# A hybrid attention layer on one core: compression MLP in two halves with its weights ahead of q_b's, first projections' banks emptied by ACT alone, k's norm weights made earlier

## The chip, the core and the metric

The kernel runs on one core of a Trainium2 chip. The metric is the device time of one execution in microseconds; before the change the median of three runs is 331.12 us (330.75 to 331.83).

## What is computed

One decoder layer on a sequence of 512 positions with 1024 channels in float32. Two groups of 8 heads of 64 attend side by side: group A with a sliding window and sinks, group B with three branches (compressed, selected, window). Cut to what matters here:

```python
h = rms_norm(x, norm_gain) * (1 + scale) + shift            # scale, shift, gate from c @ w_ada
proj = h @ w_in      # q_a|k_a|v_a|z_a | q_b|kc|vc|ks|vs|kw|vw|z_b|g_b
qa = qk_norm(q_a, q_gain_a) * qscale;  ka = qk_norm(k_a, k_gain_a)
o_a = banded_gqa(qa, ka, v_a, 128, bias_a, sinks)
k_cmp = qk_norm(compress_blocks(kc, pos_k, w_cmp_k1, w_cmp_k2), k_gain_cmp)
v_cmp = compress_blocks(vc, pos_v, w_cmp_v1, w_cmp_v2)
# compress_blocks: 31 overlapping blocks of 32 positions, silu(flat @ w1) @ w2, flat has 32*64 = 2048 inputs
o_b = sum of three gated branches (compressed, selected, window) with q_b
out = x + gate * (concat(o_a * silu(z_a), o_b * silu(z_b)) @ w_out)
```

## The kernel before

**Split products.** Each projection is made of three matmuls per tile of 128 channels: activations and weights are split into a rounded high part and the rest (`hh`, `hl` and `wh`, `wl`), and the products high x high, high x low and low x high are summed in a PSUM bank. For the weights, `split` (L161) lets ACT copy the high part (L171) and DVE subtract (L172). A weight group comes in two loads of 128x4x256 (`raw`) and is split in four parts; a split of a load's last part calls `load_next` (L147), which issues the next load of the list `raw_order` (L140 to L144) on SP's queue. The ring of raw buffers has ten places after the build, and a load waits on SP until the buffer's last reader is done; what stands behind it on SP waits too.

**Phase one** (L300 to L434) makes `h` and the first projections (q, k and v of group A) tile by tile: for each of 8 tiles DVE or PE sums the modulation (`mod_dve`, `mod_pe`), PE turns it into a column (`mod_col`, L260), DVE and ACT make `hh` and `hl`, and `first_proj` (L291) adds 24 matmuls into six banks: `sq` 0 to 3 (q of the four blocks of 128 positions) and `skv` 0 and 1 (k and v). An instruction order written by hand (`in_order`) holds in this phase. At its end DVE makes `kg` (L428 to L433), the products of q's and k's gains.

**Emptying the banks** (L437 to L451): ACT squares q (L441), copies v (L445) and half of q (L450); DVE copies k (L444) and the other half of q (L448). `prep_a` (L570) sums the squares (L573), and for k squares the copy on ACT (`sumsq`, L511, L514); `rnorm` makes the inverse root (L521 and L101 to L108); `k_scale` (L547) scales k with `kg` and splits it, PE transposes it (L560), ACT and DVE copy the transposes (L564, L565); `q_scale` (L524) does the like for q (L527 to L544).

**Phase two.** A scheduler orders each engine's instructions from the program's order and its own costs; `block()` (L495) only fixes PE's order within attention. The program is written as one stream of projections (`gen1`, `gen2`: kv_cmp, kv_sel, kv_win_g, q_b, z) that `run` (L970) advances by an amount per attention step; small tasks hang on the stream as `posts`, of which one step is taken per stream step. `cmp_mlp` (L607) is such a task: 16 steps of the 2048 inputs, each with one matmul for k and one for v of 64 columns (L614), in four quarters of four steps with one task step after each; after each quarter it calls `load_next` twice. Its sums stay in one of the two score banks (`ph`) until L622 has read them. Its weights are the loads `cmp0` (k) and `cmp1` (v), a quarter each: two quarters of both stand ahead of q_b's first two loads in `raw_order`, two behind.

## Time and profile before

| | us |
|---|---|
| median of three runs | 331.12 |
| profiled execution, whole | 331.1 |
| its span, first to last instruction | 328.9 |
| PE busy | 320.3 (97%) |
| DVE busy | 225.5 (69%) |
| ACT busy | 197.8 (60%) |
| matmuls | 2304 |

Times of instructions are counted from the span's start; 2.2 us of the execution lie outside the span. The granted TensorE clock is full throughout. Matmuls overlap: a matmul of 256 columns shows 0.28 us, but the next starts 0.12 us after it, so lengths of PE work are read from start to start. "Idle" in a row is the time in which the engine did nothing before it, and the name behind the arrow is what ended it.

### The profile page before, as it was taken

To read this page: it belongs to the slowest core of one execution; us is meant where nothing else is said; L and a number is where in the kernel's file an instruction comes from. 1 tells how busy PE (TensorE), PEld (TensorE's weight loads), DVE (VectorE), ACT (ScalarE), POOL (GpSimd) and SP (SyncE) were. 2 spreads that over 40 slices of the span, in tenths; PEclk is the share of its full clock that TensorE was granted. 3 is DMA by queue.
4 is the path that set the end of the run, shared out by engine and by line. 5 is a ranking of instruction groups with operands and counts; after the bars stand their busy time and mean duration, and the time that the engine had idled before them with its cause. 6 is when DMAs were issued, how large, how long until landed. Compare 5 with 4: busy or idle time off the path is not lost.

```text
span 328.9 us, 6232 instructions
## 1 busy us (share of the span) xinstructions
PE 320.3 (97%) x2304; PEld 262.9 (80%) x2304; DVE 225.5 (69%) x661; ACT 197.8 (60%) x478; POOL 4.6 (1%) x22
## 2 busy tenths in 40 slices
PE   8999999999999899999999999999999999999995
PEld 3577888879999779999977778678788788788884
DVE  3557697999896248787899799686576784543320
ACT  5674645656887355994967758878487586421200
POOL 1000000000000000000000000000000000000000
PEclk9999999999999999999999999999999999999999
DMA  7999966600050883122042260535240022152321
GB/s 222 388 408 410 397 222 182 247 0 3 3 159 0 276 282 117 32 65 67 32 129 81 78 229 3 190 123 200 66 128 2 0 67 64 34 161 69 123 64 64
DMA packets 31062, 44.27 MB, mean 135 GB/s; under 512 B 1767, under 2 KB 23399, under 8 KB 31033
## 3 DMA queue, kind: packets, MB, share of 16 engines
q1 hardware_dynamic: 29880, 41.79, 37.4%
q10 hardware_dynamic: 1152, 2.10, 2.2%
q8 instruction: 18, 0.29, 0.4%
q14 instruction: 12, 0.09, 0.1%
HBM read 41.74 MB, written 2.14 MB: 133 GB/s over the span
## 4 chain that ended last, share of the span: by engine, by line
PE 83%; DVE 7%; ACT 6%; DMA 2%; issue 1%; SPq 0%; ACTq 0%; DVEq 0%
PE pj L489 31%; PE sq L296 7%; PE pj L479 7%; PE s L878 6%; PE po L953 6%; PE pt L936 4%; PE skv L297 3%; PE skv L322 3%; PE pt L926 3%; PE s L614 2%; DMA raw<-in_w_cmp 2%; ACT pa L890 2%; PE pj L229 2%; PE po L959 1%; PE pj L715 1%
## 5 line engine op out<-in xcount | busy, mean ns | idle before, releaser
L171 ACT ACTIVATE wh<-raw 128x512 fp32r<-128x512 f32 (+1 forms) x52 | 31.4, 631 | 38.0 <-PE pj L489 31.5
L172 DVE TENSOR_TENSOR wl<-raw,wh 128x512 fp32r<-128x512 f32 (+1 forms) x52 | 35.1, 692 | 12.2 <-ACT wh L171 10.6
L479 PE MATMUL pj<-wl,hh 128*128 128x256 f32 (+1 forms) x128 | 36.9, 288 | 0.8 <-DVE wl L172 0.8
L479 PE MATMUL pj<-wh,hh 128*128 128x256 f32 (+1 forms) x128 | 37.1, 291 | 0.1
L479 PE MATMUL pj<-wh,hl 128*128 128x256 f32 (+1 forms) x128 | 37.0, 289 | 0.0
L890 ACT ACTIVATE pp<-pp,nm 128x256 f32<-128x256 f32 (+2 forms) x48 | 29.3, 612 | 10.9 <-DVE nm L883 10.8
L489 PE MATMUL pj<-hh,wh 128*128 128x512 f32 x80 | 32.4, 406 | 0.0
L489 PE MATMUL pj<-hl,wh 128*128 128x512 f32 x80 | 31.8, 397 | 0.0
L489 PE MATMUL pj<-hh,wl 128*128 128x512 f32 x80 | 31.6, 395 | 0.0
L883 DVE CUSTOM_DVE_ANT_0 pp<-s,bias 128x256 f32<-128x256 f32 (+2 forms) x48 | 25.4, 551 | 8.6 <-PE s L878 8.4
L489 PE MATMUL pj<-yh,wh 128*128 128x512 f32 x64 | 25.5, 399 | 0.0
L489 PE MATMUL pj<-yh,wl 128*128 128x512 f32 x64 | 25.3, 395 | 0.0
L489 PE MATMUL pj<-yl,wh 128*128 128x512 f32 x64 | 25.2, 394 | 0.0
L479 PEld LDWEIGHTS pj<-wl,hh 128*128 128x128 f32 x128 | 24.1, 188 | 1.3 <-DVE wl L172 1.0
L479 PEld LDWEIGHTS pj<-wh,hh 128*128 128x128 f32 x128 | 24.0, 188 | 1.0 <-issue 0.5
L479 PEld LDWEIGHTS pj<-wh,hl 128*128 128x128 f32 x128 | 24.1, 188 | 0.6 <-issue 0.6
L878 PE MATMUL s<-kTb,qs 128*128 128x256 f32 (+2 forms) x96 | 23.2, 359 | 0.0
L1037 DVE SCALAR_TENSOR_TENSOR fin<-pj,gate,xr 128x512 f32<-128x512 f32 x8 | 6.0, 751 | 24.6 <-PE pj L489 24.6
L911 DVE TENSOR_SCALAR pp<-pp,rr,grev 128x256 f32<-128x256 f32 (+2 forms) x48 | 21.0, 476 | 0.5
L883 DVE CUSTOM_DVE_ANT_0 pa<-s,bias,nsink 128x256 f32<-128x256 f32 (+1 forms) x32 | 14.2, 448 | 10.1 <-PE pj L479 4.4
L927 ACT COPY ptT<-pt 128x512 f32<-128x512 f32 (+1 forms) x28 | 15.3, 547 | 7.2 <-PE pt L926 7.0
L489 PEld LDWEIGHTS pj<-hh,wh 128*128 128x128 f32 x80 | 15.0, 188 | 4.7 <-issue 2.1
(241 smaller groups left out, 724.9 us busy)
## 6 DMA issues: line engine op xcount, KB each, us to landing
ada_ring<-in_w_ada_ss SPq DMA_DIRECT2D x16, 512.0 KB, 7.2
raw<-in_w_cmp SPq DMA_DIRECT2D x8, 512.0 KB, 6.7
raw<-in_w_gate SPq DMA_DIRECT2D x8, 512.0 KB, 3.8
raw<-in_w_o SPq DMA_DIRECT2D x8, 512.0 KB, 3.9
wst_ring<-in_w_qkv_a SPq DMA_DIRECT2D x8, 384.0 KB, 8.1
xTp<-in_xT SPq DMA_DIRECT2D x8, 256.0 KB, 5.4
bias<-line_d SPq DMA_DIRECT2D x8, 256.0 KB, 4.1
raw<-in_w_q_b SPq DMA_DIRECT2D x4, 512.0 KB
```

The costliest lines, as they stand in the source:

```text
L171: ACT.activation(wh, src, AF.Copy)
L172: DVE.tensor_tensor(wl, src, wh.bitcast(F32), op=OP.subtract)
L296: PE.matmul(pj_q[tb], lt, w[:, 0:512], start=f, stop=l, skip_group_check=True)
L479: PE.matmul(bank[:, t * n:(t + 1) * n], h[:, tb * 128:(tb + 1) * 128], w[:, k % 2, :], start=k == 0 and m == 0, stop=k == 7 and m == 2)
L489: PE.matmul(bank, w, h, start=k == 0 and m == 0, stop=k == 7 and m == 2)
L878: PE.matmul(ps, qs[h][:, 128 * i:128 * i + 128], k[:, hl_, lo:lo + w], start=hl_ == 0, stop=hl_ == 1)
L883: DVE.tensor_tensor_reduce(out=P[:, g, 0:w], in0=ps, in1=bt, scale=1.0, scalar=init, op0=OP.add, op1=OP.min, accum_out=nm[:, g:g + 1])
L890: ACT.activation(P[:, g, 0:e], P[:, g, 0:e], AF.Exp, bias=nm[:, g:g + 1], scale=-1.0, accum_out=dn[:, g:g + 1])
L911: DVE.tensor_scalar(v, v, rr[:, g:g + 1], gates[:, g, br:br + 1], op0=OP.mult, op1=OP.mult)
L927: ACT.copy(T[:, :, 0:nb, :], rev(pt[:, 0:2 * nb * 128].rearrange("p (g b q) -> p g b q", g=2, b=nb)))
L936: PE.transpose(pt[:, b * 128:(b + 1) * 128], P[:, g, b * 128:(b + 1) * 128], ident)
L953: PE.matmul(o[64 * g:64 * g + 64, 128 * i:128 * i + 128], vb[:, 64 * g:64 * g + 64], sl["T"][g][:, b, :], start=first_of and b == 0, stop= ...
```

## The change

- `raw_order`: all eight loads of the MLP's weights stand ahead of q_b's.
- `cmp_mlp` runs in two halves of eight steps, each one uncut `block()`; `load_next` is called twice after each fourth step, within the block. Before the second half it passes eight task steps (`WAIT_M`).
- Emptying: ACT does all of it. It squares the four q banks, squares k straight from its two banks into the new tile `ksq`, copies k, then q, then v. `prep_a` sums `ksq`; the squaring of k's copy is gone.
- The six operations on `kg` stand at the head of phase one's sixth round (`k == 5`), and `kg` becomes a part of the tile `rest`.

The diff, from the old kernel to the new:

```diff
@@ -27,7 +27,7 @@
 GW = 280
 AHEAD = 6
 NT2 = 38
-WAIT_L = 4
+WAIT_L, WAIT_M = 4, (0, 8)
 PER_A, PER_B = 3.6, (3.5, 1.6, 7)
 ND = (24, 8, 3)
 NR = 4
@@ -111,7 +111,7 @@
 
     first = con.tile([128, 168], F32, name="first")
     cT, prm, ident = first[:, 0:8], first[:, 8:40], first[:, 40:168]
-    rest = con.tile([128, 960], F32, name="rest")
+    rest = con.tile([128, 1216], F32, name="rest")
     sml, anti = rest[:, 0:416], rest[:, 416:544]
     pos = rest[:, 544:576].rearrange("p (a b) -> p a b", a=2)
     w2 = rest[:, 576:832].rearrange("p (a b d) -> p a b d", a=2, b=2)
@@ -126,7 +126,7 @@
     hl = [T2(F32R, f"hl{k}") for k in range(8)]
     gacc = con.tile([128, D], F32, name="gacc")
     line_d = dram.tile([2, 8, LINE], F32, name="line_d")
-    kg = con.tile([128, 4, HD], F32, name="kg")
+    kg = rest[:, 960:1216].rearrange("p (a d) -> p a d", a=4)
     nsink = con.tile([128, 8], F32, name="nsink")
     sc_col = con.tile([128, 8], F32, name="sc_col")
     prm1 = con.tile([128, 8], F32, name="prm1")
@@ -138,9 +138,8 @@
 
 
     raw_order = [(g, h) for g in ("kv_cmp", "kv_sel", "kv_win_g") for h in range(2)]
-    raw_order += [(f"cmp{kv}", q) for q in range(2) for kv in range(2)] + [("q_b0", 0), ("q_b0", 1)]
-    raw_order += [(f"cmp{kv}", q) for q in range(2, 4) for kv in range(2)]
-    raw_order += [(g, h) for g in ("q_b1", "z_a0", "gate0", "z_a1", "gate1", "z_b0", "gate2", "z_b1", "gate3",
+    raw_order += [(f"cmp{kv}", q) for q in range(4) for kv in range(2)]
+    raw_order += [(g, h) for g in ("q_b0", "q_b1", "z_a0", "gate0", "z_a1", "gate1", "z_b0", "gate2", "z_b1", "gate3",
                                    "o0", "o1", "o2", "o3") for h in range(2)]
     raws, pieces, pending = {}, {}, list(raw_order)
 
@@ -313,7 +312,7 @@
         for k in range(NR):
             load_ada(k)
             load_wst(k)
-        SP.dma_start(rest, A["rest"])
+        SP.dma_start(rest[:, 0:960], A["rest"])
         DVE.memset(scz, 0.0)
 
 
@@ -415,6 +414,13 @@
             elif k == LW:
                 for _ in range(5):
                     load_next()
+            if k == 5:
+                DVE.tensor_tensor(kg[:, 0], qga, kga, op=OP.mult)
+                DVE.tensor_tensor(kg[:, 1], qgb, kgs, op=OP.mult)
+                DVE.tensor_tensor(kg[:, 2], qgb, kgw, op=OP.mult)
+                DVE.tensor_tensor(kg[:, 3], qgb, kgc, op=OP.mult)
+                DVE.tensor_scalar(kg[:, 0:3], kg[:, 0:3], -(HD ** -0.5), None, op0=OP.mult)
+                DVE.tensor_scalar(kg[:, 3], kg[:, 3], HD ** -0.5, None, op0=OP.mult)
             for n in range(3):
                 first_proj(k, n)
                 for m in MOD_AFTER.get((k, n), ()):
@@ -425,29 +431,23 @@
                     new_tile(m)
                 if k >= 6 and n == 1:
                     split_to("kv_cmp", 2 * (k - 6) + 1, 0)
-        DVE.tensor_tensor(kg[:, 0], qga, kga, op=OP.mult)
-        DVE.tensor_tensor(kg[:, 1], qgb, kgs, op=OP.mult)
-        DVE.tensor_tensor(kg[:, 2], qgb, kgw, op=OP.mult)
-        DVE.tensor_tensor(kg[:, 3], qgb, kgc, op=OP.mult)
-        DVE.tensor_scalar(kg[:, 0:3], kg[:, 0:3], -(HD ** -0.5), None, op0=OP.mult)
-        DVE.tensor_scalar(kg[:, 3], kg[:, 3], HD ** -0.5, None, op0=OP.mult)
         DVE.tensor_scalar(nsink, sinks, -1.0, None, op0=OP.mult)
 
     mp = ctx.enter_context(tc.tile_pool(name="mp", bufs=1))
     qraw = mp.tile([128, NB, 512], F32, name="qraw")
     qsq = [T2(F32, f"qsq{tb}") for tb in range(NB)]
     kraw = T2(F32, "kraw").rearrange("p (t n) -> p t n", t=NB)
+    ksq = T2(F32, "ksq").rearrange("p (t n) -> p t n", t=NB)
     for tb in range(NB):
         ACT.activation(qsq[tb], pj_q[tb], AF.Square)
-        if tb % 2:
-            p = tb // 2
-            DVE.tensor_copy(kraw[:, 2 * p:2 * p + 2], pj_kv[p][:, :, 0:128])
-            ACT.activation(va[:, 2 * p:2 * p + 2, :], pj_kv[p][:, :, 128:256], AF.Copy)
+    for p in range(2):
+        ACT.activation(ksq[:, 2 * p:2 * p + 2], pj_kv[p][:, :, 0:128], AF.Square)
+    for p in range(2):
+        ACT.activation(kraw[:, 2 * p:2 * p + 2], pj_kv[p][:, :, 0:128], AF.Copy)
     for tb in range(NB):
-        if tb % 2:
-            DVE.tensor_copy(qraw[:, tb], pj_q[tb])
-        else:
-            ACT.activation(qraw[:, tb], pj_q[tb], AF.Copy)
+        ACT.activation(qraw[:, tb], pj_q[tb], AF.Copy)
+    for p in range(2):
+        ACT.activation(va[:, 2 * p:2 * p + 2, :], pj_kv[p][:, :, 128:256], AF.Copy)
     st.close()
 
     ps_px = ctx.enter_context(tc.tile_pool(name="ps_px", bufs=1, space=PSUM))
@@ -571,7 +571,7 @@
         ss = sm.tile([128, 40], F32, name="ss_a")
         for tb in range(NB):
             DVE.tensor_reduce(ss[:, 8 * tb:8 * tb + 8], qsq[tb].rearrange("p (b d) -> p b d", d=HD), AX.X, OP.add)
-        sumsq(ss[:, 32:40], kraw.rearrange("p t n -> p (t n)"), 8, True)
+        DVE.tensor_reduce(ss[:, 32:40], ksq.rearrange("p t (g d) -> p (t g) d", d=HD), AX.X, OP.add)
         rn = rn_a[0] = rnorm(ss, 40)
         yield 0.0
         yield from k_scale(0, kraw, rn[:, 32:40])
@@ -606,16 +606,19 @@
 
     def cmp_mlp():
         ph = ps_s.tile([128, 512], F32, name="s")
-        for q in range(4):
+        for half in range(2):
+            for _ in range(WAIT_M[half]):
+                yield 0.0
             with block():
-                for i in range(4):
-                    ii = 4 * q + i
+                for ii in range(8 * half, 8 * half + 8):
                     for kv in range(2):
-                        PE.matmul(ph[64 * kv:64 * kv + 64, 0:256], X[kv][:, ii // 8, :, :, ii % 8].rearrange("p g n -> p (g n)"),
-                                  raws[f"cmp{kv}", q][:, i, :], start=ii == 0, stop=ii == 15, skip_group_check=True)
-            yield 1.9
-            load_next()
-            load_next()
+                        PE.matmul(ph[64 * kv:64 * kv + 64, 0:256], X[kv][:, half, :, :, ii % 8].rearrange("p g n -> p (g n)"),
+                                  raws[f"cmp{kv}", ii // 4][:, ii % 4, :], start=ii == 0, stop=ii == 15,
+                                  skip_group_check=True)
+                    if ii % 4 == 3:
+                        load_next()
+                        load_next()
+            yield 3.6
         th_ = W2("cth", (128, 256))
         ACT.activation(th_, ph[:, 0:256], AF.Tanh, scale=0.5)
         sh = W2("csh", (128, 256))
```

**What moves on SP's queue.** The weight loads around the MLP; `raw` is the ring's buffer (with the tile's number), `in_w_cmp0` and `in_w_cmp1` are the MLP's weights for k and v, `bias` is group B's bias. Before:

```order
L152 DMA raw_961<-in_w_cmp1 128x4x256
L152 DMA raw_1048<-in_w_q_b0 128x4x256
L152 DMA raw_1094<-in_w_q_b0 128x4x256
L152 DMA raw_1273<-in_w_cmp0 128x4x256
L152 DMA raw_1344<-in_w_cmp1 128x4x256
L152 DMA raw_1346<-in_w_cmp0 128x4x256
L841 DMA bias_1397<-line_d_94 128x512
L152 DMA raw_1383<-in_w_cmp1 128x4x256
L152 DMA raw_1385<-in_w_q_b1 128x4x256
```

and with the change:

```order
L151 DMA raw_961<-in_w_cmp1 128x4x256
L151 DMA raw_1048<-in_w_cmp0 128x4x256
L151 DMA raw_1304<-in_w_cmp1 128x4x256
L151 DMA raw_1306<-in_w_cmp0 128x4x256
L151 DMA raw_1316<-in_w_cmp1 128x4x256
L151 DMA raw_1318<-in_w_q_b0 128x4x256
L844 DMA bias_1421<-line_d_94 128x512
L151 DMA raw_1369<-in_w_q_b0 128x4x256
L151 DMA raw_1379<-in_w_q_b1 128x4x256
```

q_b's two first loads moved from behind the fourth MLP load to behind the eighth, with the bias load now between them. In the new program q_b's first load waits for the reader of `raw_961` (the MLP's first half), its second for the reader of `raw_1048` (the third quarter).

**What moves on PE at the MLP.** `s<-raw,pp` are the MLP's matmuls (the trace counts two for each), `pj` those of projections, `pt` transposes, `s<-kT,qs` scores. Before, the third quarter:

```order
L878 MATMUL s<-kT_749,qs_917 128x256 x2
L614 MATMUL s<-raw,pp 64x256
L479 MATMUL pj<-wh,hl_88 128x280
L479 MATMUL pj<-wh,hh_81 128x280
L479 MATMUL pj<-wl,hh_81 128x280
L479 MATMUL pj<-wh,hl_89 128x280
L479 MATMUL pj<-wh,hh_82 128x280
L479 MATMUL pj<-wl,hh_82 128x280
L479 MATMUL pj<-wh,hl_90 128x280
L479 MATMUL pj<-wh,hh_83 128x280
L479 MATMUL pj<-wl,hh_83 128x280
L479 MATMUL pj<-wh,hl_91 128x280
```

and its other seven matmuls behind that; the fourth quarter is cut the same way, after one matmul. With the change, the second half, from its first instruction on:

```order
L615 MATMUL s<-raw,pp 64x256 x16
L929 MATMUL pt<-first,pa 128x128 x4
L881 MATMUL s<-kT_749,qs_955 128x256 x2
L479 MATMUL pj<-wh,hh_77 128x256
L479 MATMUL pj<-wl,hh_77 128x256
L479 MATMUL pj<-wh,hl_85 128x256
L629 MATMUL pt<-first,csh 128x128 x2
L479 MATMUL pj<-wh,hh_78 128x256
L881 MATMUL s<-kT_751,qs_971 128x256 x2
L479 MATMUL pj<-wl,hh_78 128x256
L479 MATMUL pj<-wh,hl_86 128x256
L479 MATMUL pj<-wh,hh_79 128x256
```

Quarters three and four are one piece now, and q_b's first matmuls (`hh_77`, 128x256) follow at once.

**What moves on PE ahead of kv_sel.** The first transposes of group A's k (`pt<-ident_r,kc`) and the matmuls around them. Before:

```order
L489 MATMUL pj<-hl_92,wh 128x512
L489 MATMUL pj<-hh_84,wl 128x512
L479 MATMUL pj<-wh,hh_77 128x256
L560 MATMUL pt<-ident_r,kc 128x128 x4
L479 MATMUL pj<-wl,hh_77 128x256
L479 MATMUL pj<-wh,hl_85 128x256
```

and with the change:

```order
L489 MATMUL pj<-hh_78,wl 128x512
L489 MATMUL pj<-hh_79,wh 128x512
L489 MATMUL pj<-hl_87,wh 128x512
L560 MATMUL pt<-ident_r,kc 128x128 x4
L489 MATMUL pj<-hh_79,wl 128x512
L489 MATMUL pj<-hh_80,wh 128x512
L489 MATMUL pj<-hl_88,wh 128x512
```

They stood behind the first of kv_sel's matmuls (L479), now within the second bank of kv_cmp's (L489), 32 of its 48 matmuls done.

## Rows read from the trace of the kernel before

**Rows 1.** The page, part 1 (busy time of each engine with its share of the span and its instructions) and part 4 (the chain that ended last, by engine):

```profile
PE 320.3 (97%) x2304; PEld 262.9 (80%) x2304; DVE 225.5 (69%) x661; ACT 197.8 (60%) x478; POOL 4.6 (1%) x22
...
PE 83%; DVE 7%; ACT 6%; DMA 2%; issue 1%; SPq 0%; ACTq 0%; DVEq 0%
```

**Rows 2.** The table of stretches of 10 us: length, then busy time (and instructions) of PE, its weight loads, DVE, ACT and POOL, the granted TensorE clock, the DMA share and GB/s:

```profile
70.00:80.00 10.00, 9.10 (x78) 8.63 (x77) 9.56 (x19) 7.49 (x18) 0.00 (x0) 1.00 0.01 2
90.00:100.00 10.00, 9.77 (x74) 8.97 (x72) 9.50 (x35) 8.39 (x26) 0.38 (x2) 1.00 0.44 133
110.00:120.00 10.00, 8.63 (x56) 6.75 (x54) 4.49 (x13) 5.42 (x14) 0.38 (x2) 1.00 0.94 316
140.00:150.00 10.00, 9.74 (x93) 9.41 (x94) 8.02 (x26) 8.13 (x21) 0.19 (x1) 1.00 0.25 71
```

**Rows 3.** The timelines of DVE and PE around 74 us. In this and the next groups: start and duration in us, engine, line, operation, out<-in; in brackets the idle time before and what ended it:

```profile
73.40 0.69 DVE L172 TENSOR_TENSOR wl<-raw,wh 128x512 fp32r<-128x512 f32 x1
...
74.14 0.38 PE L479 MATMUL pj<-wl,hh 128*128 128x256 f32 x1 [0.83 <-DVE wl L172]
```

**Rows 4.** PE's timeline through the compression MLP (L614), the attention product of group A (`po`), transposes and scores between; last, a row of the chain of waits (start, duration, line, count) with kv_sel's matmuls:

```profile
104.56 2.01 PE L614 MATMUL s<-raw,pp 128*64 128x256 f32 x16
...
107.92 1.90 PE L614 MATMUL s<-raw,pp 128*64 128x256 f32 x16
109.76 0.66 PE L926 MATMUL pt<-first,pa 128*128 128x128 f32 x4
...
110.49 0.29 PE L479 MATMUL pj<-wh,hl 128*128 128x280 f32 x1
...
113.15 0.71 PE L614 MATMUL s<-raw,pp 128*64 128x256 f32 x2 [1.30 <-DMA raw<-in_w_cmp]
113.79 0.40 PE L479 MATMUL pj<-wh,hl 128*128 128x280 f32 x1
...
115.27 2.00 PE L614 MATMUL s<-raw,pp 128*64 128x256 f32 x14
117.21 0.66 PE L926 MATMUL pt<-first,pa 128*128 128x128 f32 x4
...
119.15 0.71 PE L614 MATMUL s<-raw,pp 128*64 128x256 f32 x2
119.79 0.38 PE L479 MATMUL pj<-wh,hl 128*128 128x256 f32 x1
...
120.10 2.00 PE L614 MATMUL s<-raw,pp 128*64 128x256 f32 x14
122.04 0.39 PE L479 MATMUL pj<-wh,hh 128*128 128x256 f32 x1
...
78.03 4.08 PE pj L479 x33
```

**Rows 5.** SP's queue: two issues for q_b's first weights (start, and the time from the first issue to the end of the second); then three groups of weight loads by the tile that they fill, each with durations of the issue in ns (min/median/max), first and last start, and the time from issue to landing in us:

```profile
93.16 13.96 SPq L152 DMA_DIRECT2D raw<-in_w_q_b  x2
...
L152 SPq DMA_DIRECT2D raw<-in_w_gate x1: 545/545/545, 144.8 to 144.8; - x1
...
DMA to landing us min/median/max: 3.8/3.8/3.8
...
L152 SPq DMA_DIRECT2D raw<-in_w_cmp x1: 625/625/625, 107.2 to 107.2; - x1
...
DMA to landing us min/median/max: 5.9/5.9/5.9
...
L152 SPq DMA_DIRECT2D raw<-in_w_cmp x3: 556/913/1152, 54.0 to 55.9; - x3
...
DMA to landing us min/median/max: 8.0/8.8/8.9
```

**Rows 6.** ACT and DVE while the first projections' banks are emptied and the norms of q and k are made; last, the chain of waits' row of kv_cmp's matmuls (start, duration, line, count):

```profile
58.02 1.09 ACT L441 ACTIVATE qsq<-sq 128x512 f32<-128x512 f32 x2 [0.59 <-PE sq L296]
...
60.42 0.70 ACT L445 ACTIVATE va<-skv 128x256 f32<-128x256 f32 x2
60.95 0.67 ACT L450 ACTIVATE qraw<-sq 128x512 f32<-128x512 f32 x1
...
67.39 0.63 ACT L171 ACTIVATE wh<-raw 128x512 fp32r<-128x512 f32 x1 [4.22 <-issue]
...
61.22 2.46 DVE L573 TENSOR_REDUCE ss_a<-qsq 128x8 f32<-128x512 f32 x4
...
65.47 0.18 DVE L101 TENSOR_SCALAR n_y<-ss_a 128x40 int32<-128x40 int32 x1
...
67.35 0.69 DVE L550 TENSOR_TENSOR kn<-kraw,n_y 128x512 f32<-128x512 f32 x1
...
59.16 10.93 PE pj L489 x47
```

**Rows 7.** The end of phase one: the last tile's modulation sum on DVE (L222) and its column product on PE (L260), and the norm weights on DVE (L428, first of six, to L434, the next one behind them):

```profile
51.87 0.42 DVE L222 TENSOR_TENSOR macc<-macc,macc 128x256 f32<-128x256 f32 x1
...
52.89 0.50 PE L260 MATMUL pj<-ones,macc 128*128 128x1 f32 x4
...
58.45 0.22 DVE L428 TENSOR_TENSOR kg<-rest 128x64 f32<-128x64 f32 x1
...
59.27 0.16 DVE L434 TENSOR_SCALAR nsink<-rest 128x8 f32<-128x8 f32 x1
```

## The prediction

> **What bounds the kernel now.** I read the page's busy times and its chain of waits first, then the table of 10 us stretches, then PE's timeline where that table shows PE idle. PE is busy for 97% of the span and carries 83% of the chain that ended last [rows 1]: the kernel ends when PE's queue does, and a change can shorten it only where PE stands still or passes slowly. The change adds and removes no matmul. In the stretches [rows 2] PE's gaps are few: 0.90 us in 70 to 80, 1.37 us in 110 to 120, and 0.23 and 0.26 us in the two others shown. Two of them have a name. At 74.14 PE waited 0.83 us for the low half of the last quarter of kv_sel's weights, which DVE began only at 73.40, behind other work without a gap [rows 3]. At 113.15 it waited 1.30 us for the third quarter of the compression MLP's weights [rows 4]. The queue of SP tells why [rows 5]: q_b's second half stands ahead of that quarter and waits for a buffer that the MLP's first quarter still reads, so the first SP row has 13.96 us for two issues, and the MLP's three loads are issued only from 107.18 on.
>
> A third cost hides in "busy" time. The MLP's matmuls use 64 of the 128 columns. Sixteen in a row take 109.76 - 107.92 = 1.84 us, 0.115 each. Where such a piece stands between ordinary matmuls it takes longer: two take 113.79 - 113.15 = 0.64 us and again 119.79 - 119.15 = 0.64, fourteen take 117.21 - 115.27 = 1.94 and 122.04 - 120.10 = 1.94 [rows 4]. That is 0.41 and 0.33 us over the bare matmuls: each visit to the narrow form costs about 0.37 us. There are five visits now (the first quarters share one with the `po` matmuls between them).
>
> **The change, part by part.** The sum is made against the profiled execution, 331.1 us with a span of 328.9; the median of the runs is 331.12, so nothing has to be carried over.
>
> *MLP weights ahead of q_b's.* In the new order of SP the last four MLP loads stand ahead of q_b's first; their buffers are those of kv_cmp, kv_sel and the first win_g half, whose splits are over by about 92 us. The four loads then land by about 100, even at the 5.9 us of the load that was issued at 107.18 [rows 5]; the MLP begins at about 104. The 1.30 us go. **-1.30**; some of it stays only if a load takes over 12 us.
>
> *The MLP in halves.* The new order of PE has two uncut blocks of 16 rows (32 matmuls in the trace), the first still joined to `po`: two visits instead of five, 3 x 0.37. **-1.1** (from 3 x 0.33 to 3 x 0.41).
>
> *q_b's loads, which pay for it.* q_b's first half now waits for the MLP's first half to end; between the two blocks PE has over 4 us of other matmuls and then the second block of 3.7 us, so a load of 3.8 us, as the gate's weights took [rows 5], and a split of 0.63 + 0.69 fit. The second half is issued only when the third quarter's matmuls are over. From there PE has the fourth quarter with the way out of the narrow form (1.84 + 0.19), four transposes with a score pair (110.49 - 109.76 = 0.73), a second pair with two transposes (about 0.55, by the same row) and twelve q_b matmuls of 256 columns (0.12 each from 4.08 over 33): 4.75 us [rows 4]. The load needs 3.8 us if nothing is ahead of it, ACT's high part 0.63, hand-overs about 0.1: 4.5 us. So it just fits. With the 5.9 us of the load at 107.18, which had another ahead of it, PE would wait 1.9 us [rows 5]. I take **+0.3**, near the lower end, because the new queue has nothing ahead of this load but one bias load issued some 4 us before; bounds 0 and 1.9.
>
> *The first projections' banks, ACT alone, squares first.* Removed from DVE: two copies of k and two of q. Added to ACT: two squares of 256 (in place of one of 512 from SBUF), two k copies, two q copies. ACT sat idle for 4.22 us behind this work before [rows 6], so the longer work has room. What moves is the chain to the norms. Four squares at 0.55 and two at 0.35 end near 61.2; DVE's last reduction ends 0.6 later (2.46 for four), the root takes 67.35 - 65.47 = 1.9 us, so k is scaled from about 63.8 instead of 67.35 [rows 6]. Everything behind it (k's transposes, q's, the first scores) stands earlier in PE's new order. The last kv_sel part is still split late: thirteen DVE instructions of 0.6 to 0.7 after the first split at 64.5, so near 73.2. But PE now has 20 q transposes and three score pairs ahead of the matmul that needs it, and comes there near 75.6. **-0.83**; bounds 0 and -0.83.
>
> *The price of the early place.* k's transposes stood behind the first kv_sel matmul, now behind 32 of the 48 kv_cmp matmuls. At 10.93/47 = 0.233 us each [rows 6] PE comes there at 59.28 + 7.44 = 66.7. The first half of k is ready when ACT has emptied twelve pieces, split one weight part, DVE has done three operations and ACT one more: 66.4 if ACT's pieces overlap as in the shown rows, 67.4 if they take their full 0.55 and 0.35 one after the other. **+0.3**; bounds 0 and 1.1, since the low half, the q transposes and the first scores are as tight.
> Before, the emptying was split over both engines and over at 60.95 + 0.67 = 61.6 [rows 6]; ACT alone will be done near 64. The Trainium skill (TensorEngine Tiling (Array Packing), PSUM Bottleneck) advises to use both ScalarE and VectorE to empty PSUM. By that rule the sum loses another 2.2 us; by the rows above, where no bank is asked for before 66.7, it loses nothing from the banks themselves.
>
> *k's norm weights in phase one.* The six DVE operations take 59.27 - 58.45 = 0.82 us [rows 7] and now stand before the seventh tile's weight split. DVE has no gap from there to 52.3, so the last tile's modulation sum, which ends at 51.87 + 0.42 = 52.29, ends at 53.11. PE took it up at 52.89 [rows 7], so PE waits 0.22 us and a hand-over. **+0.28**; bounds 0 and 0.82. At the old place the same 0.82 us come off DVE, which is in the -0.83 above.
>
> Sum: -1.30 - 1.1 - 0.83 + 0.3 + 0.3 + 0.28 = -2.35, so 331.1 - 2.35 = **328.7 us**. With all best ends it is 331.1 - 1.30 - 1.23 - 0.83 = 327.7. With the three costs at their worst ends (1.9 + 1.1 + 0.82 in place of 0.88) it is 331.6; half of that way, 330.1, ends the forecast's own range, 327.7 to 330.1. Behind 130 us the order differs in detail, but the work on every engine is the same, and PE is full.
>
> **The rivals.**
> *The waits re-form (same).* If ACT alone is the narrow place, as the rule above has it, k's chain is late by the 2.2 us by which the emptying ends later, and PE, which now stands in front of k's transposes, waits for it there and at the first scores. For it: PE's margin there is 0.3 us. Against: no bank is asked for before 66.7, and the 2.2 us count in full only if each later hand-over is as tight as the first. Time: 328.7 - 0.3 + 2.2 = 330.6.
> *q_b comes late (slower).* One mechanism: PE reaches q_b's third part and its weights are not there. The place is the first q_b bank pair, behind the second MLP block; PE's queue is in order, so scores and transposes behind it wait too. It decides from a landing time of 6.65 us on: there the wait is 6.65 + 0.73 - 4.75 = 2.65 us, which is the whole gain without its own 0.3. The three loads issued from 54 us on took 8.0 to 8.9 us, with other transfers ahead of them [rows 5]; at 8.8 the wait is 8.8 + 0.73 - 4.75 = 4.8 us and the time 328.7 - 0.3 + 4.8 = 333.2. For it: five more loads are issued right behind this one. Against: the lone gate load took 3.8.
> *More is freed (faster).* The MLP's sums hold one of the two score banks from 104.56 to 122; in two blocks they hold it some 4 us less, and DVE is four copies lighter before the first scores. If the small gaps at 90 to 100 and 140 to 150 [rows 2] close as well (0.49) and the two tight places cost nothing (0.3 each): 328.7 - 0.5 - 0.6 = 327.6.
>
> **How the numbers follow.** About 0.3% (1 us) is what a measurement of this kernel can tell from no change. Forecast 0.57, waits re-form 0.17, q_b late 0.11, more freed 0.15. Faster by over 0.3% are the forecast and the last: 0.72; same 0.17; slower 0.11. The range leaves out q_b late and the outer edges: 327.2 to 331.0.
>
> **What would show it.** Right: no PE gap with the MLP's weights as releaser; two L615 pieces of 32 matmuls; no wait on `wl` in 70 to 76; the second column product of phase one (L259) some 0.3 us late at 53; PE at most some 0.5 us idle before k's transposes near 66.7 and before the first `wh` of q_b's second half. Wrong: a PE gap of over 2 us at either of these two places, a new gap on DVE's scores between 75 and 104, or an unchanged count of pieces.

## The result

The changed kernel takes 329.59 us (median; 328.65 to 330.63), the kernel before beside it 331.27: a ratio of 0.9943 with an interval of 0.9927 to 0.996, so 1.7 us less by the medians (1.3 to 2.4 by the interval). Timed again later, beside other kernels, it took 329.34 us against 331.59 (0.9925, 0.990 to 0.995). The forecast was 328.7 with a range of 327.2 to 331.0.

The profiled execution of the changed kernel is one of its slowest: 330.63 us, span 328.6. It holds a stretch of half clock, told at the end, that costs 1.55 us and that most executions of it do not have. What PE waited for, first in the kernel before, then in the changed one (engine, what waited, what it waited for; in total, times, longest, us; from 57 to 290 us):

```profile
PE s L614 <- DMA raw<-in_w_cmp: 1.3, 1, 1.3
PE pj L479 <- DVE wl L172: 0.8, 1, 0.8
PE s L878 <- DVE nm L883: 0.5, 2, 0.4
PE pt L536 <- DVE qc L531: 0.3, 1, 0.3
```

```profile
PE s L881 <- DVE nm L886: 0.8, 2, 0.6
PE s L855 <- ACT gacc L721: 0.4, 1, 0.4
PE pj L479 <- ACT wh L170: 0.3, 1, 0.3
PE pt L560 <- ACT kc L554: 0.3, 1, 0.3
PE pt L929 <- DVE pa L918: 0.2, 1, 0.2
```

The page's busy times and its chain of waits of the changed kernel, answering [rows 1]:

```profile
PE 320.7 (98%) x2304; PEld 263.2 (80%) x2304; DVE 224.1 (68%) x657; ACT 198.3 (60%) x483; POOL 4.5 (1%) x22
...
PE 76%; DVE 13%; ACT 5%; DMA 3%; issue 2%; POOL 0%; DVEq 0%; ACTq 0%; POOLq 0%
```

PE's busy time holds the half clock and so shows no gain; more of the chain runs over DVE than before (13% against 7). Both waits that the forecast named are gone, but four new ones of 0.2 to 0.4 us stand there: 2.9 us became 2.0, where the two that went are worth 2.1. In a second trace of the same kernel (after_again, below) two of the four stand (`kc` and `pa`), and the sum is 1.3. The changed kernel's stretches that answer to [rows 2] (same columns):

```profile
70.00:80.00 10.00, 9.93 (x80) 9.29 (x80) 9.79 (x20) 6.38 (x15) 0.00 (x0) 1.00 0.01 2
90.00:100.00 10.00, 10.00 (x80) 9.81 (x79) 7.72 (x26) 6.36 (x21) 0.19 (x1) 1.00 0.83 274
110.00:120.00 10.00, 9.76 (x94) 8.64 (x90) 4.80 (x18) 6.78 (x20) 0.56 (x3) 1.00 0.36 113
140.00:150.00 10.00, 10.00 (x95) 9.28 (x93) 7.91 (x29) 7.92 (x22) 0.49 (x2) 1.00 0.33 105
```

PE is fuller in all four (8.63 became 9.76 in 110 to 120), and the last four of the MLP's loads, which used to be issued from 107 us on, are now issued by 92.6 and fill 90 to 100 (133 GB/s became 274). PE's timeline at the places that the forecast named, answering [rows 3, 4, 6, 7]: the late column product, k's first transposes, the two MLP blocks, and q_b's third weight part:

```profile
53.47 0.61 PE L259 MATMUL pj<-ones,macc 128*128 128x1 f32 x4
...
66.94 0.40 PE L489 MATMUL pj<-hl,wh 128*128 128x512 f32 x1
67.27 0.53 PE L560 MATMUL pt<-ident_r,kc 128*128 128x128 f32 x4
...
100.66 0.54 PE L560 MATMUL pt<-ident_r,kc 128*128 128x128 f32 x4 [0.31 <-ACT kc L554]
...
106.00 3.74 PE L615 MATMUL s<-raw,pp 128*64 128x256 f32 x32
109.57 1.70 PE L956 MATMUL po<-ptT,va 128*64 128x128 f32 x28
...
115.09 3.74 PE L615 MATMUL s<-raw,pp 128*64 128x256 f32 x32
118.76 0.66 PE L929 MATMUL pt<-first,pa 128*128 128x128 f32 x4
...
122.12 0.51 PE L479 MATMUL pj<-wh,hh 128*128 128x256 f32 x2 [0.32 <-ACT wh L170]
```

Two pieces of 32, no wait for the MLP's weights, 0.32 us in front of q_b's second half, nothing in front of k's transposes near 67. The MLP's queue, answering [rows 5] (start, and the time from the first issue to the end of the last), and the time from issue to landing of q_b's second load:

```profile
54.69 2.13 SPq L151 DMA_DIRECT2D raw<-in_w_cmp  x3
...
88.70 3.88 SPq L151 DMA_DIRECT2D raw<-in_w_cmp  x5
109.78 0.54 SPq L151 DMA_DIRECT2D raw<-in_w_q_b  x1
...
117.12 1.89 SPq L151 DMA_DIRECT2D raw<-in_w_q_b  x3
...
DMA to landing us min/median/max: 4.3/4.3/4.3
```

### The profile page after: what moved, and what is told of

It is laid out like the page before. It is cut to its first block, busy times and chain, and to the rows that moved or that the text cites. A ratio compares the mean times of both kernels' runs of the same rounds, so it can differ in the third digit from the quotient of the medians.

```text
span 328.6 us, 6247 instructions
## 1 busy us (share of the span) xinstructions
PE 320.7 (98%) x2304; PEld 263.2 (80%) x2304; DVE 224.1 (68%) x657; ACT 198.3 (60%) x483; POOL 4.5 (1%) x22
## 4 chain that ended last, share of the span: by engine, by line
PE 76%; DVE 13%; ACT 5%; DMA 3%; issue 2%; POOL 0%; DVEq 0%; ACTq 0%; POOLq 0%
PE pj L489 28%; PE pj L479 7%; PE s L881 7%; PE po L956 6%; PE sq L295 5%; PE pt L939 4%; PE pt L929 3%; PE skv L321 3%; PE skv L296 2%; DVE wl L171 2%; PE s L615 2%; DMA raw<-in_w_z_b 2%; DMA raw<-in_w_q_b 1%; PE pj L228 1%; PE po L962 1%
## 5 line engine op out<-in xcount | busy, mean ns | idle before, releaser
L479 PE MATMUL pj<-wh,hl 128*128 128x256 f32 (+1 forms) x128 | 37.1, 290 | 0.0
L479 PE MATMUL pj<-wh,hh 128*128 128x256 f32 (+1 forms) x128 | 36.6, 287 | 0.3 <-ACT wh L170 0.3
L479 PE MATMUL pj<-wl,hh 128*128 128x256 f32 (+1 forms) x128 | 36.6, 287 | 0.0
L489 PE MATMUL pj<-hh,wh 128*128 128x512 f32 x80 | 32.5, 407 | 0.0
L489 PE MATMUL pj<-hh,wl 128*128 128x512 f32 x80 | 31.8, 398 | 0.0
L489 PE MATMUL pj<-hl,wh 128*128 128x512 f32 x80 | 31.8, 397 | 0.0
L489 PE MATMUL pj<-yl,wh 128*128 128x512 f32 x64 | 26.1, 407 | 0.0
L489 PE MATMUL pj<-yh,wh 128*128 128x512 f32 x64 | 26.0, 409 | 0.0
L489 PE MATMUL pj<-yh,wl 128*128 128x512 f32 x64 | 25.9, 404 | 0.0
L479 PEld LDWEIGHTS pj<-wh,hh 128*128 128x128 f32 x128 | 24.0, 188 | 0.6 <-ACT wh L170 0.5
L479 PEld LDWEIGHTS pj<-wl,hh 128*128 128x128 f32 x128 | 24.0, 188 | 0.2 <-issue 0.2
L479 PEld LDWEIGHTS pj<-wh,hl 128*128 128x128 f32 x128 | 24.1, 188 | 0.1
L489 PEld LDWEIGHTS pj<-hh,wh 128*128 128x128 f32 x80 | 15.0, 188 | 5.7 <-issue 3.0
```

Source lines behind the costliest of these rows:

```text
L479: PE.matmul(bank[:, t * n:(t + 1) * n], h[:, tb * 128:(tb + 1) * 128], w[:, k % 2, :], start=k == 0 and m == 0, stop=k == 7 and m == 2)
L489: PE.matmul(bank, w, h, start=k == 0 and m == 0, stop=k == 7 and m == 2)
```

## The experiments

**How they are read.** From one execution to the next the same first instructions end at other times: the second group of sixteen modulation products (L228 of the changed kernel, L229 before) starts at 18.66 us in the trace of the kernel before, at 18.96 and 19.53 in the two of the changed one, at 18.57 to 19.96 over all. So beside the medians the table has the length from there to the start of the last matmul, from one trace each (for the changed kernel both traces, less 1.55 us of half clock each), and the start of kv_cmp's first matmul, counted from the same product. "Waits" is the sum of PE's named waits from 57 to 290 us, as printed in tenths, "visits" the visits to the 64-column form, "MLP" what its 64 matmuls (as the trace counts them) take, from start to start. Six of the changed kernel's twenty executions hold the half clock; without them its two medians are 329.5 and 329.1.

| kernel | median | ratio to before | length | kv_cmp | waits | visits | MLP |
|---|---|---|---|---|---|---|---|
| before | 331.3 to 331.6 | | 306.2 | 40.33 | 2.9 | 5 | 8.81 |
| the change | 329.6, 329.3 | 0.9943, 0.9925 | 304.1, 303.3 | 40.79, 40.80 | 2.0, 1.3 | 2 | 7.24 |
| mlp_only | 328.8 | 0.990 (0.986 to 0.994) | 303.4 | 40.35 | 2.0 | 2 | 7.24 |
| loads_only | 329.0 | 0.992 (0.989 to 0.995) | 303.6 | 40.35 | 1.9 | 3 | 7.56 |
| front_only | 327.9 | 0.9875 (0.984 to 0.991) | 302.4 | 40.80 | 1.1 | 3 | 7.56 |
| front_both | 331.8 | 0.9996 (0.997 to 1.003) | 305.8 | 40.80 | 2.3 | 5 | 8.82 |
| kg_late | 328.1 | 0.988 (0.984 to 0.992) | 302.3 | 40.33 | 1.4 | 2 | 7.24 |
| kg_early | 328.0 | 0.990 (0.987 to 0.993) | 302.9 | 40.45 | 1.5 | 2 | 7.24 |
| both_empty | 328.7 | 0.991 (0.988 to 0.994) | 302.7 | 40.80 | 1.3 | 2 | 7.24 |
| qb_early | 329.5 | 0.994 (0.991 to 0.996) | 303.9 | 40.78 | 1.2 | 3 | 7.87 |
| front_kg3 | 328.2 | 0.988 (0.985 to 0.991) | 302.6 | 40.47 | 1.5 | 3 | 7.56 |
| front_kg3_halves | 328.7 | 0.989 (0.986 to 0.992) | 303.0 | 40.43 | 1.9 | 2 | 7.24 |
| eight_pieces | 331.4 | 0.998 (0.996 to 1.000) | 306.0 | 40.79 | 2.3 | 4 | 7.78 |

**mlp_only**: the kernel before with the new load order and the two halves, and nothing else.

```diff
+    raw_order += [(f"cmp{kv}", q) for q in range(4) for kv in range(2)]
...
+        for half in range(2):
```

> The kernel before with the MLP's part alone: its weights loaded ahead of q_b's and its two halves; emptying and norm weights stay as they were. Theory (the gain is the MLP's): -1.30 for the wait, -1.1 for the visits, +0.3 for q_b's second load, so 2.1 us less than before, 329.2 us; the 0.83 us wait for kv_sel's low part near 74 us stays in the trace. Rival (the front part carries the gain, or the two only pay together): less than 1 us of gain, 330.3 us or more.

It takes 328.79 us, 2.8 less than before and 0.55 less than the whole change beside it (0.3 less than its executions without half clock; the length, 303.4, lies among the change's two). So nothing shows that the rest of the change adds to it. The MLP's part earns more than forecast, and there is no wait in front of q_b's third part. kv_sel's low part is late as before; that row of its timeline answers the last one of [rows 3]:

```profile
74.70 0.39 PE L478 MATMUL pj<-wl,hh 128*128 128x256 f32 x1 [0.86 <-DVE wl L171]
```

**front_only**: the other half of the change, with the loads in their old order and the MLP in quarters.

```diff
+            if k == 5:
+                DVE.tensor_tensor(kg[:, 0], qga, kga, op=OP.mult)
...
+    for p in range(2):
+        ACT.activation(ksq[:, 2 * p:2 * p + 2], pj_kv[p][:, :, 0:128], AF.Square)
...
     for tb in range(NB):
...
+        ACT.activation(qraw[:, tb], pj_q[tb], AF.Copy)
```

> The kernel before with the front part alone: ACT empties the banks, squares first, norm weights in phase one; MLP in quarters and loads in the old order. Theory: -0.83 (the wait near 74 us goes), +0.28 (macc late at the end of phase one), +0.3 or less (k's transposes), so 0.25 to 0.55 us less than before, 330.7 to 331.0 us, hardly to be told from before; the 1.3 us wait for the MLP's third quarter stays. Rival (ACT alone is the narrow place and waits re-form): 332 us or more. Rival (more freed): 330.0 or less.

It takes 327.88 us, 3.7 less than before: the rival that more is freed, and with kg_late, kg_early and front_kg3 (328.0 to 328.2) the fastest of the kernels here. The 1.3 us wait, which the theory left in place, is gone. The queue of SP says why:

```profile
88.84 0.56 SPq L152 DMA_DIRECT2D raw<-in_w_cmp  x1
89.51 1.24 SPq L152 DMA_DIRECT2D raw<-in_w_q_b  x2
90.84 16.32 SPq L152 DMA_DIRECT2D raw<-in_w_cmp  x4
107.21 1.84 SPq L152 DMA_DIRECT2D raw<-in_w_q_b  x2
```

q_b's two loads are issued within 1.24 us where they took 13.96 [rows 5]. In the built program q_b's second load has got the raw buffer of a kv_cmp load, free by then; in the kernel before it has that of the MLP's first quarter, while two other buffers that no one reads any more go to the loads behind it. Which buffer a load gets is settled when the kernel is built, and the new emptying shifts that. The traces name no buffers; what they show is the wait: in the kernel before the load is issued at 106.62 us, when the matmuls of the first quarter are over (104.56 + 2.01), in front_only at once. PE's order in this build also leaves the quarters uncut (8, 8, 8, 8 instructions): three visits.

**after_again**: the changed kernel a second time.

> The changed kernel once more, for a second trace. In the first trace matmuls ran at half clock for 1.67 us near 282 us and for 0.4 us more than before in the first 5 us; without both its span would be 326.5, yet the median of the runs is 329.6 with a span of some 327.5. Theory (run-to-run differences sit in the landing of q_b's second load, 4.29 us in the first trace, and in the clock): in this trace the wait in front of q_b's third part differs from 0.32 us by as much as the landing differs from 4.29. Rival (they sit elsewhere): the same landing and another place with 0.5 to 1 us of new idle time. Time 329.6 us, 329.0 to 330.2.

The wait in front of q_b's third part is smaller (0.25 us over the normal spacing, 0.48 in the first trace), and the one for `gacc` (0.60 in the first trace) is gone; together some 0.8 us, what the two lengths differ by. So theory and rival each hold a part. The half clock is there again.

**kg_late**: the changed kernel with the six operations back behind phase one.

```diff
-            if k == 5:
-                DVE.tensor_tensor(kg[:, 0], qga, kga, op=OP.mult)
...
+        DVE.tensor_tensor(kg[:, 0], qga, kga, op=OP.mult)
```

> The changed kernel with the six operations on k's norm weights back behind phase one. Theory: the column product of the last tile is no longer late, -0.28, and DVE carries 0.82 us more while the norms are made, where k's transposes had no idle time in front of them in the trace: 0 to +0.8 there. Together -0.3 to +0.5, so 329.3 to 330.1 us. In the trace: no late column product near 53 us, and idle time in front of k's first transposes near 66 us if that place is as tight as predicted (0.3 us of margin), none if it has more slack. Rival (the move is what makes the early place possible): over 0.5 us slower than the changed kernel.

328.10 us, 1.2 less than the changed kernel beside it; outside the expectation, and against its rival. kv_cmp starts 0.46 us earlier, as in the kernel before. The price behind it is there too, at q's transposes instead of k's:

```profile
74.39 0.54 PE L535 MATMUL pt<-ident_r,qc 128*128 128x128 f32 x4 [0.59 <-DVE qc L530]
```

Yet its length is 1.0 and 1.8 us below those of the change's two traces. With that wait taken at 74 us, those for `pa` near 89 us and for `kc` near 101, which both traces of the change have, do not occur; those at 122.12 and for `gacc` do not either, but the second trace of the change has hardly any of these. Named waits (1.4 us against 2.0 and 1.3) and kv_cmp's 0.46 explain a part of it.

**loads_only**: the kernel before with the two lines of `raw_order` alone (as in mlp_only's diff, MLP in quarters).

> The kernel before with only the order of the loads changed: all eight loads of the MLP's weights ahead of q_b's, MLP in quarters. In this kernel's PE queue the four quarters come out uncut (8, 8, 8, 8 instructions; three visits to the narrow form instead of five, two instead of three with the halves). Theory (the order of the loads is what earns): -1.30 for the wait, -0.78 for two visits of 0.39, +0.25 to 0.48 for q_b's second load, so 1.6 to 1.8 us less than before, 329.7 us, and the run with the halves as well (328.8) is one visit, 0.39 us, and a bit faster. Rival (the halves are needed): 330.5 us or more.

329.01 us: the order of the loads alone earns 2.3 of the 2.8 us. The quarters come out uncut by themselves. The third visit that the halves save is worth 0.2 us here, which the spread of the runs does not set apart from nothing.

**qb_early**: the changed kernel with q_b's first two loads ahead of the MLP's last quarter.

```diff
+    raw_order += [(f"cmp{kv}", q) for q in range(3) for kv in range(2)] + [("q_b0", 0), ("q_b0", 1)]
+    raw_order += [(f"cmp{kv}", 3) for kv in range(2)]
```

> The changed kernel with q_b's two first loads ahead of the MLP's last quarter. q_b's weights then have no buffer to wait for; in PE's queue the second MLP block is cut once (9 and 7 instructions), so there is one visit more. Theory: the wait in front of q_b's third part (0.48 and 0.25 us over the normal spacing in the two traces of the changed kernel) goes, the visit costs 0.39: -0.1 to +0.15 us against the changed kernel, 329.3 us. Rival (q_b's late load costs more than these waits, by what stands behind it): 328.8 us or less. Rival (the last quarter's weights now come late): 330 us or more with a wait of the MLP for a load.

329.50 us, as expected: the wait goes, the visit comes (MLP 7.87 against 7.24, because this cut falls within a step, as told below).

**kg_early**: the changed kernel with `if k == 3:` for the norm weights.

> The changed kernel with the six operations on k's norm weights two rounds earlier, where DVE had gaps of 0.4 to 1.0 us between its instructions. The build gives this kernel twelve raw buffers instead of ten, and q_b's loads wait for no reader of the MLP. Theory: the late column product goes (-0.46 at the start of kv_cmp's matmuls, by the traces), and so does the wait in front of q_b's third part (-0.25 to -0.48): 0.7 to 0.9 us less than the changed kernel, 328.5 us. Rival (DVE's gaps there are on the path of the next tile): the 0.46 stays or moves to an earlier tile, 329.0 or more.

327.98 us, below the expectation by 0.5. kv_cmp starts 0.34 us earlier than in the change and PE does not wait for q_b. Twelve raw buffers and the earlier place can't be told apart in this run alone.

**both_empty**: the changed kernel with the copies shared again.

```diff
-        ACT.activation(kraw[:, 2 * p:2 * p + 2], pj_kv[p][:, :, 0:128], AF.Copy)
+        DVE.tensor_copy(kraw[:, 2 * p:2 * p + 2], pj_kv[p][:, :, 0:128])
...
+        if tb % 2:
+            DVE.tensor_copy(qraw[:, tb], pj_q[tb])
```

> The changed kernel with DVE taking over k's two copies and two of q's four again (squares still first, on ACT). Theory: ACT alone is not the narrow place, since PE had no idle time in front of k's transposes in either trace; the four copies, some 2 us, stand on DVE, which is full from 60 to 80 us, so its low parts come later and PE waits up to 0.8 us there: 329.4 to 330.2 us. Rival (the rule that both engines should empty the banks): the chain to k's transposes and all behind it is up to 2 us earlier, and the time is 328.8 us or less.

328.70 us: at the rival's edge. The wait for kv_sel's low part is back (0.6 us), as the theory has it, but the waits for `kc` and `pa` (0.5 us), which both traces of the change have, and for `wh` and `gacc`, which the first has (0.7), are not there. Emptying on ACT alone moved waits; it did not lower their sum. The run is not a clean test of the emptying: in this build q_b's first two loads also start earlier, at 96.78 and 113.97 us against 109.78 and 117.12, which by itself can take the wait for `wh` away. The interval (0.988 to 0.994) overlaps that of the change, so a gain of some 0.6 us is likely, not certain, and its cause is not shown.

**front_both**: the front part alone, with the copies shared. It tells whether front_only's gain is the emptying or the buffer.

> The kernel before with the front part alone, but with k's copies and half of q's left on DVE: only the order (squares first), k's squares from the banks and the early norm weights are new; loads and quarters as before. In this build q_b's second load gets a buffer that the MLP's first quarter still reads, as in the kernel before; in the front part with ACT alone (327.9 us) it got one of kv_cmp's and did not wait. Theory (the front part's gain is that other buffer, through the 1.30 us wait and the two visits): the 1.3 us wait and the five visits are back, kv_sel's low part is late by 0.8 us as in the run with both engines, the norm weights cost 0.46: 331.3 to 332.0 us. Rival (the emptying itself earns, by the early chain of k and q): 329.5 us or less.

331.83 us, ratio 0.9996: nothing is left of the 3.7 us. SP's queue and PE's wait are like those of the kernel before; q_b's second load is again issued when the first quarter's matmuls end (107.7 us):

```profile
93.46 0.54 SPq L152 DMA_DIRECT2D raw<-in_w_q_b  x1
94.13 0.54 SPq L845 DMA_DIRECT2D bias<-line_d  x1
107.71 0.55 SPq L152 DMA_DIRECT2D raw<-in_w_q_b  x1
108.30 2.60 SPq L152 DMA_DIRECT2D raw<-in_w_cmp  x3
```

```profile
113.93 0.71 PE L618 MATMUL s<-raw,pp 128*64 128x256 f32 x2 [0.96 <-DMA raw<-in_w_cmp]
```

The two lengths differ by 3.4 us. Behind q_b's second load stand 2.2 of them: the wait of 0.96, and 8.82 - 7.56 = 1.26 for the cut quarters. Another 0.6 is the wait for kv_sel's low part, which comes back with DVE's copies as it does in both_empty; the last 0.6 was not traced. So the larger part hangs on where the load goes, and the emptying on ACT matters most because it changes that; a build that changes the buffer alone was not run.

**front_kg3** (front_only with `if k == 3:`) and **front_kg3_halves** (that with the MLP's halves) were to beat front_only.

> The front part alone with ACT emptying, and the norm weights two rounds earlier (twelve raw buffers in this build); loads and quarters as before. Theory: 327.9 us less the 0.3 to 0.46 us that the early norm weights cost in the sixth round: 327.5 us. Rival (the gain of that move in the changed kernel came from its buffers alone): 327.9 us.

> The same with the MLP in halves, loads in the order of the kernel before (q_b's first two loads between the MLP's second and third quarter); q_b's loads wait for no reader of the MLP. Theory: one visit less (0.39 us) than with quarters, no wait in front of q_b's third part: 327.1 us, below both kernels. Rival (the long blocks push what stands behind them by as much, as in the changed kernel): 327.9 us or more.

328.19 and 328.67 us; neither does, and both rivals hold. kv_cmp starts 0.33 us earlier, and a wait for `kc` near 100 us (0.3) takes it back. The halves make the MLP 0.32 us shorter and the kernel 0.5 longer: in every trace with halves PE waits 0.44 to 0.72 us over the normal spacing for a score bank near 138 us (0.37 to 0.39 with quarters uncut), and the wait for `gacc` occurs in traces with halves only.

**eight_pieces**: the changed kernel's MLP in eight blocks of two steps.

```diff
+        for e in range(8):
...
+                for ii in (2 * e, 2 * e + 1):
...
+            yield 0.9
```

> The changed kernel with its MLP in eight blocks, which come out as five pieces and four visits to the narrow form (the first two pieces share one with the attention product) in place of two. Theory (0.37 to 0.39 us for each visit): 0.75 to 0.8 us more than the changed kernel, 330.1 us. Rival (visits cost nothing in the sum, because the pieces in between would wait otherwise): 329.4 us.

331.40 us, some 2 us more than the changed kernel. Of it the MLP's matmuls are 7.78 - 7.24 = 0.54. Part of the rest is a wait of scores between its last two pieces (0.86 us over the normal spacing; in the changed kernel no MLP piece follows there; of the last piece the view holds the first six products):

```profile
117.26 0.48 PE L881 MATMUL s<-kT,qs 128*128 128x256 f32 x2
118.44 0.50 PE L881 MATMUL s<-kT,qs 128*128 128x256 f32 x2 [0.70 <-DVE nm L886]
118.87 0.93 PE L615 MATMUL s<-raw,pp 128*64 128x256 f32 x6
```

The MLP's sums hold one of the two score banks until the last piece is done, which is the likely reason; it was not tried by itself, and what is left of the 2 us was not traced. So a visit has a price at PE and, where scores stand between the pieces, another at the bank.

## Why the forecast held, and which of its steps did not

The direction and the size held. That the size held is in part luck: two errors of opposite sign stand in the sum.

- **-1.30, the MLP's weights: right.** The loads are issued by 92.6 us and PE does not wait.
- **-1.1, the visits: the right sign, too small, and the larger part of the mechanism was missing.** The MLP's matmuls take 8.81 us before and 7.24 now: -1.57. The step put all that a cut piece takes over the bare matmuls down to the visit. The start times show a second cost. In an uncut piece a step's matmul for k and its matmul for v run side by side: their starts are 0.006 us apart, and a pair starts every 0.216 us. In the kernel before, the cuts fell between these two matmuls, so k's stood alone in the piece of two and v's alone at the end of the fourteen. The first four products of an uncut piece take as long as the two that stood alone at 113.15 (0.71 us, [rows 4]):

```profile
104.56 0.71 PE L614 MATMUL s<-raw,pp 128*64 128x256 f32 x4
```

A cut within a step thus costs 2 x 0.216 = 0.43 us. A visit costs 0.21 in the MLP's own matmuls (what it costs the instruction in front was not summed): the second start of a piece comes 0.11 late, the instruction behind the piece 0.10. Together 32 x 0.216 + 5 x 0.21 + 2 x 0.43 = 8.82 us, against 8.81 measured (of the -1.57 the two cuts are 0.86, three visits 0.63, and a way out that now falls behind the `po` matmuls 0.10); with quarters uncut 32 x 0.216 + 3 x 0.21 = 7.54 against 7.56; in qb_early, whose cut falls within a step again, the changed kernel's 7.24 + 0.21 + 0.43 = 7.88 against 7.87. The prediction's 0.115 us as the bare matmul is also a little long, because the 1.84 us of sixteen [rows 4] hold one turn. The Trainium skill (TensorEngine Tiling (Array Packing), Key Properties) says that changing the tiling mode drains TensorE; these traces agree, at the 0.21 us above.
- **-0.83, kv_sel's low part: the wait went, the gain did not come.** It is the step that failed. mlp_only, which keeps that wait, is not slower than the whole change. Elsewhere PE now waits 0.2 us for `pa` (at 89 us), 0.3 for `kc` (at 101), 0.3 more than before for `nm` (at 115 and 139), and in the first trace 0.4 for `gacc` (at 193). The waits for `pa` and `kc` stand in both traces of the change and in none of mlp_only, kg_late and both_empty (front_only has the one for `pa`), so they seem to come with ACT's emptying and the early norm weights together. In kind that is the rival "the waits re-form", though not at the place that it named, k's transposes near 67.
- **+0.3, q_b's second load: right.** It landed after 4.29 us, and PE waited 0.32; in the second trace it landed after 4.1 and the wait was 0.1.
- **+0.3, k's transposes: 0.** PE came to them at 67.27 and did not wait; `kc`'s high half had been ready at 67.2. ACT was done with the banks at 64.46, near the forecast's 64 (the rival's 2.2 us later is 2.4 by its own two numbers), and PE did not wait for them there.
- **+0.28, the norm weights: right at their place, too small in all.** PE stood 0.28 us in front of the column product, and kv_cmp's matmuls start 0.46 late. Putting them back (kg_late) takes 1.2 us off the changed kernel, 1.0 where that ran without half clock.
- **The parts were added as if they were independent. They are not.** Each alone takes the 1.3 us wait and the two cut quarters away, one by the order of the loads (2.8 us less), the other by the buffer that q_b's second load gets (3.7 less); together they earn 1.7 to 2.3. The forecast looked at the order of the queue and took the buffer of a load for given.

With the sizes of the first trace the forecast's sum is -1.30 - 1.57 - 0.83 + 0.32 + 0.46 = -2.92 us. The waits that it had put at nothing give 0.9 of it back (net of one that went), which leaves -2.0; the length changed by -2.1. In the second trace, with 0.1 for q_b and 0.5 given back, it is -2.6 against -2.9.

What stays open: front_only's length is 0.9 to 1.7 us below the change's two, and its named waits 0.9 and 0.2 below theirs; the remainder was not traced to a place.

## What to carry to other kernels

When a load waits for a buffer, look which buffer the build gave it and whether another stood free: here the wait and the cut blocks behind that choice were worth 2.2 us, about as much as the whole change, and an edit elsewhere flipped it. Before a cut is priced, look at which instructions start together: a cut between the two of a pair costs more than the turn. Two parts that remove the same wait must not be added; run each alone. On an engine that is 97% busy, a wait removed early can come back in smaller pieces downstream, as here, so count all named waits, not the one, and in more than one trace.

## What the runs showed of the hardware

In both traces of the changed kernel TensorE's granted clock falls within the last projection, at the same place (281.4 and 281.2 us), though PE stood busy in front of it. From the table of stretches of the first trace (columns as in [rows 2]):

```profile
276.00:281.00 5.00, 5.00 (x54) 3.84 (x53) 1.77 (x3) 1.41 (x4) 0.00 (x0) 1.00 0.01 3
...
281.20:284.60 3.40, 3.40 (x12) 2.73 (x12) 3.01 (x6) 2.36 (x5) 0.00 (x0) 0.55 0.24 77
...
285.00:290.00 5.00, 5.00 (x23) 4.03 (x22) 0.96 (x2) 0.00 (x0) 0.00 (x0) 1.00 0.00 0
```

0.55 is nearly all of it at the lower level, 1.2 GHz: matmuls of 512 columns start 0.43 us apart in place of 0.23, and the stretch costs 1.55 us against the same matmuls in the kernel before. In front of it PE ran narrow products (64 and 32 columns of the array) and products of one column:

```profile
276.00 2.19 PE L956 MATMUL po<-ptT,vw 128*64 128x128 f32 x36
278.11 1.07 PE L962 MATMUL po<-ptc,vc 32*64 32x512 f32 x4
...
280.37 1.17 PE L1036 MATMUL pj<-ones,gacc 128*128 128x1 f32 x10
281.40 0.66 PE L489 MATMUL pj<-yh,wh 128*128 128x512 f32 x1
```

The same instructions run in the kernel before without a fall in its trace. The Trainium skill (TensorE: Matmul & The Clock Gate, What's actually happening) has the clock follow how busy PE has recently been; a PE that is busy by the profile's count (5.00 of 5.00 us) was not spared here. The mean granted clock of an execution shows it: 0.995 in six of twenty executions of the changed kernel (both traces are of these), 0.993 or 0.994 in nine of the 52 of the kernel before that ran beside the experiments (332.9 to 334.4 us), in two of qb_early's eight, one of both_empty's six, three of front_both's twelve (0.993), and in none of the other runs. Only the two traces show where it falls. What decides it was not tried.
